# Gate and up projections of a SwiGLU by seven half-size products (Strassen's scheme) in a hybrid decoder layer

## The chip, the core and the metric

The kernel runs on one core of a Trainium2 chip. The metric is device time in microseconds of one execution; less is better. Several executions are timed, and their median counts. Beside them one execution is profiled, and all rows below are from that one. The engines are PE (TensorE), DVE (VectorE), ACT (ScalarE), POOL (GpSimd) and SP (SyncE, which here only starts transfers).

## The reference, cut to what matters

One decoder layer over 2,048 tokens of width 1,024 in float32. Two branches (a gated DeltaNet and a sliding-window attention) are merged and added to x; then comes the feed-forward part, which the change touches:

```python
x = x + merged @ w_out
h = rms_norm(x, ffn_norm)                       # (2048, 1024)
x = x + (silu(h @ w_gate) * (h @ w_up)) @ w_down  # w_gate, w_up: (1024, 2816), w_down: (2816, 1024)
```

## The kernel before

The tokens are worked off in four blocks of 512 (`TB`). Every large product keeps float32 accuracy by splitting each operand into a high part (rounded to the matmul's float32r) and the rest: a product is three matmuls, high x high, high x low, low x high (`mm3`). `weights` brings a unit of 128 x 1,024 weights in two halves of 512 columns. In block 0 it loads them raw (`wraw`), ScalarE makes the high part (L168), VectorE or GpSimd in turn the low part (L171), both into a `whl` buffer (five of them), and SP stores this pair in device memory (`wk`, L174). In blocks 1 to 3 the pair is loaded from there (L181), 512 KB for each half. L109 is the helper through which all other instructions pass.

A block runs through these stages:

- `mixer`: projections, DeltaNet and attention of the block, gates and branch outputs.
- `tok_gemm(("wo",))`: the output projection; VectorE adds it to x (eight tiles `x`).
- `norm2`: `norm_stats` scales the rows (`xn`); `norm_T` transposes them with TensorE into one bank for each 128 of the 1,024 features (k = 0 to 7), ScalarE makes the high part `h` with the gain, VectorE the low part. In blocks 0 to 2 `window_start` of the next block (the projections `skv` and `sq`, acc<-whl,h in the rows, from that block's own `hs`) is issued meanwhile.
- the feed-forward in five parts of 4, 4, 4, 4 and 6 units of 128 channels (`FSPLIT`), 22 units a block: `ffn_up` for each unit, then the down product of the part (`tok_gemm(("down", part))`, acc<-whl,a in the rows).

`ffn_up` makes gate and up of a unit with `chan_gemm`: eight steps of 128 features, three matmuls each, 512 tokens wide, into one bank; twice 24 matmuls. ScalarE takes the tanh from the bank, VectorE multiplies, ScalarE and VectorE split the result (`a`).

TensorE's order is written out by hand: `drive` issues the dense stream and puts steps of the side programs (norms, attention of the next block, DeltaNet cores) into it where an estimate says that their operands are ready; side steps have priority on the other engines. The order on these engines is fixed at build time by a scheduler that knows the buffers. Nearly all tiles of 128 x 512 (x, h, a, th and those of attention) share one pool of 63 buffers (`NU`), and there are eight accumulator banks. `hs`, the normalized input of the next block (16 buffers), stays in that pool from before the feed-forward until the next `mixer` has used it.

Of the kernel before, what the change touches and what calls it, by code (L numbers as in the profile page):

```python
# [15 lines left out]
P = 128  # L16
# [3 lines left out]
TB = 512  # L20
# [8 lines left out]
NU = 63  # L29
ND = 6  # L30
WR = 2
WB = 5
# [82 lines left out]
class Emitter:  # L115
    def __init__(self, ctx, tc, ins, out, nblocks):
# [13 lines left out]
        self.kept = {}  # L130
        self.pacc = pool("acc", 8, space=bass.MemoryType.PSUM)
# [21 lines left out]

    def weights(self, key, a):
        nc = self.raw
        n = a * 264 if key[0] == "skv" else 1024
        h = a // 2
        hl = []
        if key not in self.kept:
            src = self.w_skv[key[1]] if key[0] == "skv" else self.w_all[UNITS[key]]  # L160
            raw = self.wp.tile([P, 1056], F32, name="wraw", tag="wraw", bufs=WR)
            nc.sync.dma_start(out=raw[:, :n], in_=src)
            keep = []
            for j in range(2):
                t = self.wp.tile([P, 2, 528], F32R, name="whl", tag="whl", bufs=WB)
                r = raw[:, j * n // 2:(j + 1) * n // 2]
                hi, lo = t[:, 0, :n // 2], t[:, 1, :n // 2]
                nc.scalar.activation(hi, r, AF.Copy)  # L168
                self.nsub += 1
                eng = nc.vector if self.nsub > 6 and self.nsub % PSUB else nc.gpsimd  # L170
                eng.tensor_tensor(out=lo, in0=r, in1=hi, op=ALU.subtract)  # L171
                if self.nblocks > 1:
                    d = self.kp.tile([P, 2, n // 2], F32, name="wk", tag="wk%d_%d" % (len(self.kept), j))
                    nc.sync.dma_start(out=d, in_=t[:, :, :n // 2].bitcast(F32))  # L174
                    keep.append(d)
                hl.append([t[:, e, :n // 2].rearrange("p (a m) -> p a m", a=h) for e in range(2)])
            self.kept[key] = keep
        else:
            for j in range(2):
                t = self.wp.tile([P, 2, 528], F32R, name="whl", tag="whl", bufs=WB)  # L180
                nc.sync.dma_start(out=t[:, :, :n // 2].bitcast(F32), in_=self.kept[key][j])  # L181
                hl.append([t[:, e, :n // 2].rearrange("p (a m) -> p a m", a=h) for e in range(2)])
        return lambda k: (hl[k // h][0][:, k % h], hl[k // h][1][:, k % h])
# [914 lines left out]
```

## Time and profile before

| | |
|---|---|
| median of 3 runs | 3191.2 us (3190.91 to 3194.72) |
| the profiled execution | 3196.1 us |
| its span, first to last instruction | 3194.3 us |
| mean granted TensorE clock | 0.990 of full speed |
| data moved by transfers | 595.99 MB, 187 GB/s on average |

The span is what the trace shows; the time of the execution holds a little more around it. "Busy" is the time in which an engine has at least one instruction running, and matmuls overlap, so the distance between the starts of two matmuls is less than the duration of one. Idle time of an engine counts only where a result waits for that engine.

### The profile page before, as it was taken

How to read it: one execution, taken by the hardware profiler on the slowest of the kernel's cores; microseconds unless marked ns; L12 is line 12 of the kernel's file. 1: busy time of each engine (PE TensorE's matmuls, PEld its weight loads, DVE VectorE, ACT ScalarE, POOL GpSimd, SP SyncE). 2: the span in 40 equal slices, each digit the busy share in tenths (PEclk: the TensorE clock that was granted, in tenths of full speed). 3: DMA queues.
4: the chain of work that ended last, by engine and by line, in shares of the span. 5: the costliest groups of instructions: out<-in, count | busy, mean ns of one | idle time of the engine just before them, and what ended most of it. 6: DMA issues, size and time to landing. Idle time of an engine off the chain costs nothing. (4 is left out here: it accounts for less than half of the span.)

```text
span 3194.3 us, 39761 instructions
## 1 busy us (share of the span) xinstructions
PE 3095.3 (97%) x14854; PEld 2523.6 (79%) x14854; DVE 1403.2 (44%) x3626; ACT 837.6 (26%) x2112; POOL 415.8 (13%) x401
## 2 busy tenths in 40 slices
PE   7888989999999999999999999999999999999999
PEld 5776778778888887878887888877888888878887
DVE  5867656533336544542215565443221655422221
ACT  4454334422323322330002323232000233110000
POOL 2433211322212100010001110011000211000000
PEclk9999999999999999999999999999999999999999
DMA  6554475588874446445556445545566544645565
GB/s 240 185 178 152 154 251 209 198 284 285 283 254 145 132 142 215 153 152 191 184 192 200 131 143 179 177 154 170 190 189 205 169 131 133 198 159 193 192 189 183
DMA packets 291848, 595.99 MB, mean 187 GB/s; under 512 B 18975, under 2 KB 20168, under 8 KB 291656
## 3 DMA queue, kind: packets, MB, share of 16 engines
q1 hardware_dynamic: 277648, 569.20, 54.1%
q10 hardware_dynamic: 14008, 24.25, 2.2%
q8 instruction: 117, 1.92, 0.2%
q14 instruction: 75, 0.61, 0.1%
HBM read 459.08 MB, written 134.30 MB: 186 GB/s over the span
## 5 line engine op out<-in xcount | busy, mean ns | idle before, releaser
L109 PE MATMUL acc<-h,whl 128*128 128x512 f32 x7296 | 1760.1, 397 | 7.5 <-DVE whl L171 4.9
L109 PEld LDWEIGHTS acc<-h,whl 128*128 128x128 f32 x7296 | 1357.6, 189 | 313.9 <-DVE whl L171 5.8
L109 PE MATMUL acc<-whl,a 128*128 128x512 f32 x2112 | 493.7, 393 | 0.0
L109 PEld LDWEIGHTS acc<-whl,a 128*128 128x128 f32 x2112 | 395.5, 188 | 90.3
L109 DVE TENSOR_TENSOR x<-x,acc 128x512 f32<-128x512 f32 x192 | 131.4, 687 | 390.4 <-PE acc L109 388.6
L171 POOL TENSOR_TENSOR whl<-wraw,whl 128x512 fp32r<-128x512 f32 (+1 forms) x123 | 167.0, 1359 | 565.4 <-ACT whl L168 472.6
L168 ACT ACTIVATE whl<-wraw 128x512 fp32r<-128x512 f32 (+1 forms) x240 | 149.0, 630 | 290.3 <-PE acc L109 136.1
L109 DVE TENSOR_TENSOR th<-th,acc 128x512 f32<-128x512 f32 x88 | 60.4, 687 | 316.0 <-PE acc L109 315.8
L109 DVE SCALAR_TENSOR_TENSOR th<-th,acc 128x512 f32<-128x512 f32 x88 | 60.5, 687 | 304.9 <-ACT th L109 304.9
L109 PE MATMUL acc<-whl,mt 128*128 128x512 f32 x768 | 181.9, 398 | 8.1 <-DVE h L109 7.6
L109 ACT ACTIVATE th<-acc 128x512 f32<-128x512 f32 x88 | 52.7, 598 | 499.5 <-PE acc L109 499.3
L109 PEld LDWEIGHTS acc<-whl,mt 128*128 128x128 f32 x768 | 145.9, 191 | 43.2 <-DVE h L109 8.5
L109 DVE SCALAR_TENSOR_TENSOR cv<-xr,cst_sb,cv 128x512 f32<-128x512 f32 x144 | 134.6, 935 | 60.7 <-ACT cv L109 53.1
L109 ACT ACTIVATE a<-th 128x512 fp32r<-128x512 f32 x88 | 55.5, 631 | 346.8 <-DVE th L109 332.1
L171 DVE TENSOR_TENSOR whl<-wraw,whl 128x512 fp32r<-128x512 f32 x117 | 89.8, 768 | 121.4 <-ACT whl L168 120.9
L109 PE MATMUL acc<-whl,h 128*128 128x264 f32 (+1 forms) x768 | 139.8, 341 | 0.0
L109 PEld LDWEIGHTS acc<-whl,h 128*128 128x128 f32 x768 | 118.0, 188 | 16.7 <-issue 1.1
L109 POOL COPY ccar<-xr 128x3 f32<-128x3 f32 x48 | 9.0, 188 | 858.5 <-ACT xr L109 858.5
L109 PE MATMUL acc<-sp,whl 128*128 128x512 f32 x384 | 103.2, 409 | 0.0
L109 POOL TENSOR_TENSOR pT<-pT,cst_sb 128x512 f32<-128x512 f32 x62 | 82.7, 1362 | 137.2 <-ACT pT L109 121.1
L109 ACT ACTIVATE L<-L,ast 128x256 f32<-128x256 f32 (+1 forms) x192 | 83.4, 457 | 60.0 <-DVE ast L109 60.0
L109 PE MATMUL acc<-ydn,whl 128*128 128x512 f32 x384 | 92.6, 401 | 0.4
(183 smaller groups left out, 2817.5 us busy)
## 6 DMA issues: line engine op xcount, KB each, us to landing
whl<-wk SPq DMA_DIRECT2D x708, 512.0 KB, 3.9
wk<-whl SPq DMA_DIRECT2D x236, 512.0 KB, 3.5
wraw<-in_w_all SPq DMA_DIRECT2D x118, 512.0 KB, 5.0
x<-in_x ACTq DMA_DIRECT2D x56, 256.0 KB, 5.1
out<-x ACTq DMA_DIRECT2D x32, 256.0 KB, 3.8
whl<-wk SPq DMA_DIRECT2D x12, 528.0 KB, 5.1
wk<-whl SPq DMA_DIRECT2D x4, 528.0 KB, 2.7
x<-in_x SPq DMA_DIRECT2D x8, 256.0 KB, 6.5
```

Of the source, the lines that this page charges most:

```text
L109: r = f(*args, **kw)
L168: nc.scalar.activation(hi, r, AF.Copy)
L171: eng.tensor_tensor(out=lo, in0=r, in1=hi, op=ALU.subtract)
```

## The change

The weights of a unit are seen as four quarters: A11 and A12 are the gate's weights for features 0 to 511 and 512 to 1,023, A21 and A22 the up's. The normalized input is seen as four quarters too: B11 and B12 are features 0 to 511 for the first and the second 256 tokens, B21 and B22 features 512 to 1,023. Eight quarter products (each four steps of 128 features, 256 tokens wide) become seven, of sums:

S1 = A21 + A22, S2 = S1 - A11, S3 = A11 - A21, S4 = A12 - S2 for the weights; T1 = B12 - B11, T2 = B22 - T1, T3 = B22 - B12, T4 = B21 - T2 for the input. `ffn_up` runs them in the order S2 T2 (bank Y), A11 B11 (bank G), S1 T1 (bank Z), S3 T3 (added into Y), A12 B21 (into G), A22 T4 (into Y), S4 B22 (into Z). Between them ScalarE copies Y and G out (`c`), and VectorE and GpSimd add the pieces to gate and up.

The sums S1 to S4 are built in block 0. S1 and S2 are stored split, S3 and S4 as plain sums (256 KB); in blocks 1 to 3 S1 and S2 are loaded split, S3, S4, A11, A12 and A22 plain, and split again each time. The input sums are built in each block by `norm_S` in place of `norm_T`. All `weights` calls now load raw halves; there are five raw buffers of half a unit (before two of a whole one), six `whl` buffers and 61 buffers in the common pool. For blocks 1 to 3 `hs` is stored in device memory after `window_start` and loaded again by `refill` during the last down product of the block before.

```diff
-NU = 63
+NU = 61
 ND = 6
-WR = 2
-WB = 5
+WR = 5
+WB = 6
+KEPT_SPLIT = ("S1", "S2")
...
+    def load_raw(self, src, n=TB):
+        raw = self.wp.tile([P, 528], F32, name="wraw", tag="wraw", bufs=WR)
+        self.raw.sync.dma_start(out=raw[:, :n], in_=src)
+        return raw[:, :n]
+    def either(self):
+        self.nsub += 1
+        return self.raw.vector if self.nsub > 6 and self.nsub % PSUB else self.raw.gpsimd
+    def split_raw(self, r, n=TB):
+        t = self.wp.tile([P, 2, 528], F32R, name="whl", tag="whl", bufs=WB)
+        hi, lo = t[:, 0, :n], t[:, 1, :n]
+        self.raw.scalar.activation(hi, r, AF.Copy)
+        self.either().tensor_tensor(out=lo, in0=r, in1=hi, op=ALU.subtract)
+        return t
+    def keep(self, t, n=TB):
+        d = self.kp.tile([P, 2, n], F32, name="wk", tag="wk%d" % self.nkept)
+        self.nkept += 1
+        self.raw.sync.dma_start(out=d, in_=t[:, :, :n].bitcast(F32))
+        return d
+    def load_kept(self, d, n=TB):
+        t = self.wp.tile([P, 2, 528], F32R, name="whl", tag="whl", bufs=WB)
+        self.raw.sync.dma_start(out=t[:, :, :n].bitcast(F32), in_=d)
+        return t
...
+    def seven(self, keys):
+        quad = lambda m, h: self.w_all[UNITS[keys[m]]][:, h * TB:(h + 1) * TB]
+        own = {"A11": (0, 0), "A12": (0, 1), "A22": (1, 1)}
+        got = {}
+        first = keys not in self.kept
+        if first:
+            self.kept[keys] = {}
+        kept = self.kept[keys]
+        def sums():
+            v, gp = self.raw.vector, self.raw.gpsimd
+            for n, (m, h) in list(own.items()) + [("A21", (1, 0))]:
+                got[n] = self.load_raw(quad(m, h))
+            for n, x, y, op, eng in (("S1", "A21", "A22", ALU.add, v), ("S2", "S1", "A11", ALU.subtract, v),
+                                     ("S3", "A11", "A21", ALU.subtract, gp), ("S4", "A12", "S2", ALU.subtract, gp)):
+                got[n] = self.u([TB], name="ws")
+                eng.tensor_tensor(out=got[n], in0=got[x], in1=got[y], op=op)
+        def of(name):
+            if first:
+                if not got:
+                    sums()
+                t = self.split_raw(got[name])
+                if self.nblocks > 1 and name in KEPT_SPLIT:
+                    kept[name] = self.keep(t)
+                elif self.nblocks > 1 and name not in own:
+                    d = self.kp.tile([P, TB], F32, name="wk", tag="wk%d" % self.nkept)
+                    self.nkept += 1
+                    self.raw.sync.dma_start(out=d, in_=got[name])
+                    kept[name] = d
+            elif name in KEPT_SPLIT:
+                t = self.load_kept(kept[name])
+            else:
+                t = self.split_raw(self.load_raw(quad(*own[name]) if name in own else kept[name]))
+            return [t[:, e, :TB].rearrange("p (a m) -> p a m", a=4) for e in range(2)]
+        return of
+    def product(self, ps, w, H, operand, start=True):
+        mm = self.nc.tensor.matmul
+        for k in range(4):
+            hi, lo = H[k][operand]
+            for i, (l, r) in enumerate(((w[0], hi), (w[0], lo), (w[1], hi))):
+                mm(ps, l[:, k], r, start=start and k == 0 and i == 0, stop=k == 3 and i == 2, skip_group_check=not start)
+            yield 0
...
+    def norm_S(self, xns, gain, H):
+        nc, v, gp = self.nc, self.nc.vector, self.nc.gpsimd
+        half = (slice(0, 256), slice(256, 512))
+        for k in range(4):
+            hf = []
+            for kk in (k, k + 4):
+                ps = self.aux()
+                for t in range(NT):
+                    nc.tensor.transpose(ps[:, t * P:(t + 1) * P], xns[t][kk // 4][:, (kk % 4) * P:(kk % 4 + 1) * P], self.ident)
+                f = self.u([2, 256], name="hf")
+                nc.scalar.activation(f.rearrange("p a n -> p (a n)"), ps, AF.Copy, scale=gain[:, kk:kk + 1])
+                hf.append(f)
+                yield 0
+            (b11, b12), (b21, b22) = [(f[:, 0], f[:, 1]) for f in hf]
+            ta, tb = [self.u([2, 256], name="hs") for _ in range(2)]
+            gp.tensor_tensor(out=ta[:, 0], in0=b12, in1=b11, op=ALU.subtract)
+            gp.tensor_tensor(out=ta[:, 1], in0=b22, in1=ta[:, 0], op=ALU.subtract)
+            v.tensor_tensor(out=tb[:, 0], in0=b22, in1=b12, op=ALU.subtract)
+            v.tensor_tensor(out=tb[:, 1], in0=b21, in1=ta[:, 1], op=ALU.subtract)
+            one = self.u([2, 256], F32R, name="hb")
+            nc.scalar.activation(one[:, 0], b11, AF.Copy)
+            v.tensor_tensor(out=one[:, 1], in0=b11, in1=one[:, 0], op=ALU.subtract)
+            o = {"B11": (one[:, 0], one[:, 1])}
+            for src, names, eng in ((hf[1], ("B21", "B22"), v), (ta, ("T1", "T2"), v), (tb, ("T3", "T4"), gp)):
+                hi, lo = [self.u([2, 256], F32R, name="hb") for _ in range(2)]
+                nc.scalar.activation(hi, src, AF.Copy)
+                eng.tensor_tensor(out=lo, in0=src, in1=hi, op=ALU.subtract)
+                for i, n in enumerate(names):
+                    o[n] = (hi[:, i], lo[:, i])
+            H.append(o)
+            yield 0
...
-    def ffn_up(self, hs, f):
-        nc, v = self.nc, self.nc.vector
-        w = self.weights(("up", f, 0), 8)
-        pg = self.acc()
-        yield from self.chan_gemm(pg, w, hs)
+    def ffn_up(self, H, f):
+        nc, v, gp = self.nc, self.nc.vector, self.nc.gpsimd
+        w = self.seven((("up", f, 0), ("up", f, 1)))
+        half = (slice(0, 256), slice(256, 512))
+        bank = lambda: self.acc()[:, 0:256]
+        Y = bank()
+        yield from self.product(Y, w("S2"), H, "T2")
+        c = self.u([2, 256], name="pc")
+        nc.scalar.activation(c[:, 1], Y, AF.Copy)
+        G = bank()
+        yield from self.product(G, w("A11"), H, "B11")
+        nc.scalar.activation(c[:, 0], G, AF.Copy)
+        U = self.u([2, 256], name="pu")
+        gp.tensor_tensor(out=U[:, 0], in0=c[:, 0], in1=c[:, 1], op=ALU.add)
+        Z = bank()
+        yield from self.product(Z, w("S1"), H, "T1")
+        yield from self.product(Y, w("S3"), H, "T3", start=False)
+        v.tensor_tensor(out=U[:, 1], in0=c[:, 0], in1=Y, op=ALU.add)
         th = self.u([TB], name="th")
-        nc.scalar.activation(th, pg, AF.Tanh, scale=0.5)
-        v.scalar_tensor_tensor(out=th, in0=th, scalar=1.0, in1=pg, op0=ALU.add, op1=ALU.mult)
-        w = self.weights(("up", f, 1), 8)
-        pu = self.acc()
-        yield from self.chan_gemm(pu, w, hs)
-        v.tensor_tensor(out=th, in0=th, in1=pu, op=ALU.mult)
+        up = self.u([TB], name="up")
+        v.tensor_tensor(out=up[:, half[1]], in0=U[:, 1], in1=Z, op=ALU.add)
+        yield from self.product(G, w("A12"), H, "B21", start=False)
+        nc.scalar.activation(th[:, half[0]], G, AF.Tanh, scale=0.5)
+        v.scalar_tensor_tensor(out=th[:, half[0]], in0=th[:, half[0]], scalar=1.0, in1=G, op0=ALU.add, op1=ALU.mult)
+        yield from self.product(Y, w("A22"), H, "T4", start=False)
+        v.tensor_tensor(out=up[:, half[0]], in0=c[:, 0], in1=Y, op=ALU.add)
+        yield from self.product(Z, w("S4"), H, "B22", start=False)
+        v.tensor_tensor(out=U[:, 0], in0=U[:, 0], in1=Z, op=ALU.add)
+        nc.scalar.activation(th[:, half[1]], U[:, 0], AF.Tanh, scale=0.5)
+        v.scalar_tensor_tensor(out=th[:, half[1]], in0=th[:, half[1]], scalar=1.0, in1=U[:, 0], op0=ALU.add, op1=ALU.mult)
+        v.tensor_tensor(out=th, in0=th, in1=up, op=ALU.mult)
...
+        if b:
+            self.put = []
+            for k, h in enumerate(hs):
+                self.put.append([])
+                for e in range(2):
+                    d = self.kp.tile([P, TB], F32, name="hk", tag="hk%d_%d" % (k, e))
+                    nc = self.raw
+                    nc.scalar.dma_start(out=d, in_=h[e].bitcast(F32))
+                    self.put[-1].append(d)
+            hs.clear()
+    def refill(self, hs):
+        for d in self.put:
+            h = self.pair("h")
+            for e in range(2):
+                self.raw.scalar.dma_start(out=h[e].bitcast(F32), in_=d[e])
+            hs.append(h)
+            yield 1500
...
-        yield lambda: kv.scales
+        yield lambda: kv.scales and len(hs) == KT
...
-            yield lambda: len(h2) == KT
+            yield lambda: len(h2) == 4
...
                 last = part == len(FSPLIT) - 1
+                if last and more:
+                    h2.clear()
+                    self.spawn(self.refill(hs))
```

## Rows read from the trace of the kernel before

**Rows 1.** The page: engine, busy us, share of the span, instructions.
```profile
PE 3095.3 (97%) x14854; PEld 2523.6 (79%) x14854; DVE 1403.2 (44%) x3626; ACT 837.6 (26%) x2112; POOL 415.8 (13%) x401
```
**Rows 2.** Groups by shape, whole run: busy us, mean ns, idle before, its enders.
```profile
L109 PE MATMUL acc<-h,whl 128*128 128x512 f32 x7296 | 1760.1, 397 | 7.5 <-DVE whl L171 4.9 <-POOL whl L171 1.3 <-DVE kd L109 1.3
...
L109 PE MATMUL acc<-whl,h 128*128 128x264 f32 x384 | 47.8, 285 | 0.0
...
L109 PE MATMUL aux<-cst_sb,R 128*128 128x128 f32 x128 | 19.7, 277 | 0.0
```
**Rows 3.** Timeline of TensorE, unbroken rows of one shape: start us, us, what.
```profile
2892.80 40.44 PE L109 MATMUL acc<-h,whl 128*128 128x512 f32 x174
...
1271.78 8.45 PE L109 MATMUL acc<-whl,h 128*128 128x264 f32 x68
...
1375.99 2.22 PE L109 MATMUL aux<-kt,qT 128*128 128x256 f32 x16
...
1003.21 1.06 PE L109 MATMUL aux<-T,bl 128*128 128x128 f32 x8
```
**Rows 4.** By stretch: us, engines' busy time (instructions), granted clock, DMA share, GB/s.
```profile
528.00:587.00 59.00, 56.29 (x272) 45.48 (x271) 35.92 (x110) 30.88 (x81) 18.34 (x18) 0.97 0.61 213
...
694.00:738.00 44.00, 44.00 (x191) 35.71 (x190) 12.72 (x19) 14.04 (x24) 11.67 (x9) 1.00 0.87 297
...
1311.00:1367.00 56.00, 55.48 (x276) 44.84 (x275) 28.95 (x103) 21.83 (x64) 8.38 (x11) 1.00 0.50 160
...
1469.00:1513.00 44.00, 44.00 (x191) 35.69 (x190) 7.57 (x11) 4.29 (x7) 0.00 (x0) 1.00 0.63 196
```
**Rows 5.** Groups by shape, four units of block 3, 2890 to 2935 us.
```profile
L109 DVE TENSOR_TENSOR th<-th,acc 128x512 f32<-128x512 f32 x4 | 2.8, 688 | 16.9 <-PE acc L109 16.9
...
L109 DVE SCALAR_TENSOR_TENSOR a<-th,a 128x512 fp32r<-128x512 f32 x3 | 2.1, 692 | 2.1 <-ACT a L109 2.1
```
**Rows 6.** Groups by shape, four units of block 0, 694 to 738 us.
```profile
L171 POOL TENSOR_TENSOR whl<-wraw,whl 128x512 fp32r<-128x512 f32 x9 | 11.7, 1297 | 36.3 <-ACT whl L168 36.3
L168 ACT ACTIVATE whl<-wraw 128x512 fp32r<-128x512 f32 x17 | 10.7, 631 | 23.2 <-PE acc L109 8.4 <-issue 6.4 <-DMA wraw<-in_w_all 5.2
L171 DVE TENSOR_TENSOR whl<-wraw,whl 128x512 fp32r<-128x512 f32 x8 | 5.5, 690 | 2.9 <-ACT whl L168 2.9
```
**Rows 7.** Groups by shape, attention in block 1, 1311 to 1447 us: 256 columns from a bank.
```profile
L109 DVE CUSTOM_DVE_ANT_0 L<-aux,bias 128x256 f32<-128x256 f32 x32 | 11.6, 420 | 1.4 <-PE aux L109 1.2
```
**Rows 8.** Timeline of block 3, end of the output projection and second norm, 2800 to 2826.
```profile
2799.69 13.33 PE L109 MATMUL acc<-whl,mt 128*128 128x512 f32 x57
...
2813.06 0.69 DVE L109 TENSOR_TENSOR x<-x,acc 128x512 f32<-128x512 f32 x1 [0.70 <-PE acc L109]
...
2817.66 6.15 PE L109 MATMUL aux<-cst_sb,xn 128*128 128x128 f32 x32 [4.64 <-DVE xn L109]
...
2819.42 0.69 ACT L109 ACTIVATE h<-aux,cst_sb 128x512 fp32r<-128x512 f32 x1 [4.92 <-PE aux L109]
...
2821.98 3.04 ACT L109 ACTIVATE h<-aux,cst_sb 128x512 fp32r<-128x512 f32 x5 [0.17 <-PE aux L109]
...
2823.57 2.81 PE L109 MATMUL acc<-h,whl 128*128 128x512 f32 x11
```
**Rows 9.** Transfers in 694 to 738 and in 1469 to 1513: median us to landing last.
```profile
wraw<-in_w_all SPq DMA_DIRECT2D x8, 512.0 KB, 5.0
...
whl<-wk SPq DMA_DIRECT2D x16, 512.0 KB, 3.8
```
**Rows 10.** By stretch in block 3, columns as in rows 4.
```profile
2818.00:2820.00 2.00, 2.00 (x9) 1.52 (x9) 2.00 (x6) 0.58 (x1) 0.00 (x0) 0.50 0.03 8
...
2822.00:2824.00 2.00, 2.00 (x18) 1.96 (x17) 1.90 (x3) 2.00 (x4) 0.00 (x0) 0.97 0.00 0
```
**Rows 11.** Instructions on tile h, block 1: ns min/median/max, first and last start us.
```profile
L109 PE MATMUL acc<-h,whl x17: 387/393/404, 1311.1 to 1314.8; 128*128 128x512 f32 x17
...
L109 DVE SCALAR_TENSOR_TENSOR h<-aux,cst_sb,h x8: 741/742/745, 1288.4 to 1293.0; 128x512 fp32r<-128x512 f32 x8
```

More of the change, by code (lines that the diff above doesn't have):

```diff
@@ L130, in __init__ @@
         self.kept = {}
+        self.nkept = 0
         self.pacc = pool("acc", 8, space=bass.MemoryType.PSUM)
@@ L154, in weights @@
+    def keep(self, t, n=TB):
[7 more added lines that the diff above has]
+        return t
     def weights(self, key, a):
-        nc = self.raw
-        n = a * 264 if key[0] == "skv" else 1024
+        n = (a * 264 if key[0] == "skv" else 1024) // 2
@@ L157, in weights @@
         h = a // 2
[L158 to L171, printed above, removed]
-                if self.nblocks > 1:
[L173 to L182, printed above, removed]
@@ L183, in weights @@
-        return lambda k: (hl[k // h][0][:, k % h], hl[k // h][1][:, k % h])
+        src = self.w_skv[key[1]] if key[0] == "skv" else self.w_all[UNITS[key]]
+        hl, kept = [], []
+        for j in range(2):
+            if key in self.kept:
+                t = self.load_kept(self.kept[key][j], n)
+            else:
+                t = self.split_raw(self.load_raw(src[:, j * n:(j + 1) * n], n), n)
+                if self.nblocks > 1:
+                    kept.append(self.keep(t, n))
+            hl.append([t[:, e, :n].rearrange("p (a m) -> p a m", a=h) for e in range(2)])
@@ new lines, in weights @@
+        if kept:
+            self.kept[key] = kept
+        return lambda k: (hl[k // h][0][:, k % h], hl[k // h][1][:, k % h])
+    def seven(self, keys):
[28 more added lines that the diff above has]
+                t = self.load_kept(kept[name])
+            else:
+                t = self.split_raw(self.load_raw(quad(*own[name]) if name in own else kept[name]))
+            return [t[:, e, :TB].rearrange("p (a m) -> p a m", a=4) for e in range(2)]
+        return of
@@ L378, in norm2 @@
         yield
-        yield from self.norm_T(xns, self.g2, hs)
+        yield from self.norm_S(xns, self.g2, hs)
         yield
```

## The prediction, made before the changed kernel ran

> **What bounds the kernel now.** I read the page first: TensorE is busy for 97% of the span, VectorE for 44% [rows 1]. Busy time alone proves little, because matmuls overlap, so I went to the groups by shape. The 7,296 matmuls that multiply `whl` with `h` (4,224 of them the gate and up products) had TensorE idle for 7.5 us in front of them in all [rows 2]. The timeline gives the distance between matmul starts: 174 matmuls of 512 columns in 40.44 us; less the duration of the last one (0.39), that is 40.05 / 173 = 231.5 ns each, with no hole [rows 3]. The table by stretch shows the other engines in the same phase: in a quiet stretch of block 1, VectorE is busy 7.6 us of 44, ScalarE 4.3 and GpSimd 0; in block 0, where weights are split, 12.7, 14.0 and 11.7 [rows 4]. TensorE is the bound and it is bound by columns streamed. So a gate/up unit (one of 22 per block, 88 in all) costs 48 x 0.2315 = 11.1 us, and the 88 cost 977.9 us.
>
> **The gain.** A unit becomes seven products of 4 x 3 = 12 matmuls over 256 columns: 84 matmuls. What one costs is the main number. Four spans are at hand [rows 3]: 512 columns 231.5 ns; 264 columns (8.45 - 0.29) / 67 = 121.8 ns, with a weight load in front of each [duration in rows 2]; 256 columns (2.22 - 0.29) / 15 = 128.7 ns, in attention, where VectorE empties each bank and waits are in it; 128 columns about (1.06 - 0.28) / 7 = 111 ns, hardly less than at twice the width, so something other than columns limits there. The line through the first two has 0.442 ns a column, and 8 columns below 264 give 118.3. I take 119, nearest to the 264 row, which is the same kind of stream. After: 88 x 84 x 0.119 = 879.6 us, a gain of 98 us. Bounds: 111 ns gives 157 us, 128.7 ns gives 27 us.
> The Trainium skill (TensorE: Matmul & The Clock Gate, Part 3, "What overlaps and what doesn't") says that a weight load overlaps matmuls in flight only where it goes to another row group; here every load takes all rows, so half-size matmuls would pay each load in full. The 264-column row contradicts it: a load per matmul, and 121.8 ns. By the rule the sum is that of rival 4, by the row the one used here.
>
> **Work added on the other engines.** VectorE before, per unit: three operations of 0.69 us [rows 5] = 2.1 us, and in block 0 two of the four splits, 1.4 us [rows 6]. After: six 256-wide operations of about 0.42 [rows 7] and two 512-wide ones of 0.69: 3.9 us. Five of the seven weight operands are now split in every block, alternately by VectorE and GpSimd: 2.5 x 0.69 = 1.7 us more, 5.6 in all. In block 0 all seven are split (2.4) and two sums are built (1.4): 7.7 us. GpSimd in block 0: 3.5 splits and two sums of 1.30 [rows 6], one 256-wide add of about 0.65: 7.8 us. ScalarE in block 0: seven splits of 0.63, the tanh as two halves, two copies, one final split (0.63): 4.4 + 2.2 = 6.6. A unit lasts 84 x 0.119 = 10.0 us, so in quiet stretches every engine fits. Their work is not free where its cover is gone, in four places:
> (a) *The accumulator is read in mid-run.* Bank `Y` is read by VectorE after the fourth product, and the sixth product adds to it. Only the fifth lies between: 12 x 0.119 = 1.43 us. VectorE starts about 0.04 us after the modelled end of the last matmul (end 2799.69 + 13.33 = 2813.02, start 2813.06 [rows 8]), which lies 0.29 - 0.12 = 0.17 us after the product's last slot; its add takes 0.42. That is 0.63, leaving 0.8 us: enough for one 0.69 us operation in front, not for two. I charge 0.05 us a unit, 4 us; bounds 0 and 0.5 us a unit (44).
> (b) *Attention of the next block runs beside the first part of the feed-forward.* In block 1's stretch VectorE was busy 28.95 us of 56 [rows 4], 8.3 of them its four units. With 4 x 5.6 instead it is 43.0 of some 51.6: 83%. In block 0: 35.92 of 59, less 4 x 3.5, plus 4 x 7.7: 52.7 of 54.6, 97%. There the queue in front of (a) is long, and u-buffers (28 for the new operands, four more per unit) are as scarce as before. I charge 6 us in block 0 and 2 in blocks 1 and 2: 10; bounds 0 and 40.
> (c) *Sums of weights in block 0.* The operand `S2` of the next unit needs A21, and A21's buffer (one of five) comes free when A12 of the present unit has been split, which waits for the `whl` buffer (one of six) that is freed 1.4 us before this unit begins. From there: split 0.63 + 1.30, load 4 to 5 (512 KB took 5.0 in block 0, 3.8 later [rows 9]), S1 and S2 0.7 each, split 0.63 + 0.69 or 1.30: 8.6 to 10.3 us, of 11.4 available, queues and signals not counted. With VectorE and GpSimd about 78% busy, some waits of 0.3 us eat that. I charge 0.3 us a unit, 6 us; bounds 0 and 1.5 (33).
> (d) *The norm before the feed-forward.* It prepares 28 tiles instead of 16. ScalarE's share is five 512-wide operations per k and one half: at (3.04 - 0.69) / 4 = 0.59 us apart [rows 8], 3.25 us, for four k 13 us, against 4.7 before. In block 3 nothing covers it. There ScalarE began at 2819.42 and TensorE's first product at 2823.57 [rows 8]; the first new product needs T2 of all four k, at 2819.4 + 13 + 0.7 = 2833.1, where unhindered it would end at 2823.6 + 1.4 = 2825.0: +8 us. TensorE idles meanwhile. After the idle 4.64 us before these transposes the granted clock was 0.50, that is 1.2 GHz, and back at 2.4 GHz after 2822 [rows 8, 10]; some 5 us of work at half speed cost 2.5 us. Together 10.5; bounds 5 and 16. In blocks 0 to 2 the projections of the next block cover it: `h` was finished at 1293.0 + 0.7 and first used at 1311.1 [rows 11], 17 us of room for 8.3 more. But the 61 u-buffers do not hold everything (x1 8, xn 8, hs 16, H 28, k and v 5, four in the making: 69), so the fourth k waits until the query projection has released eight of `hs`, half way through its 96 x 0.2315 = 22 us. That still fits; 1 us each, 3; bounds 0 and 15.
>
> **Costed at nothing.** DMA: a unit of blocks 1 to 3 loads 2 x 512 + 5 x 256 KB = 2.25 MB in 10.0 us, 225 GB/s, against 2 MB in 11.1; block 0 moves 2.5 MB, 250 GB/s, and carried 297 at a share of 0.87 [rows 4]. The load of a kept operand has five products, 7.1 us, for the 3.8 of [rows 9]. If that cover went, TensorE would wait for `whl`. The 4 MB of `hs` go out during the projections and come back during the last down product (144 x 0.2315 = 33 us, so 120 GB/s, beside 12 loads of 512 KB, 190), on ScalarE's queue, where at that time nothing else is queued but the output stores, which nobody waits for. 1 us in all.
>
> **Sum.** -98 + 4 + 10 + 6 + 10.5 + 3 + 1 = -64 us. The profiled execution took 3196.1 us (span 3194.3), so 3132; the median of the runs is 4.9 us below it, so the prediction is 3127 us.
>
> **Rivals.**
> 1. *Nothing stalls.* The other engines are ordered well ahead, as in block 0 now, where VectorE's and GpSimd's splits kept TensorE idle for 4.9 + 1.3 us in all [rows 2]. For it: all averages are below 100%. Against: (a) leaves 0.8 us where before nothing on TensorE waited for an evacuation. Time: 3191 - 98 + 10 = 3103. Chance 0.17.
> 2. *The read of `Y` comes late in every unit* (the other side). VectorE is served in a fixed order; if each time two operations or one waiting split stand in front, TensorE loses about 1 us a unit. It decides from (64 + 4) / 88 = 0.77 us a unit on; at 1 us the time is 3127 - 4 + 88 = 3211, slower. For it: VectorE has eight operations a unit and 1.7 us of splits that wait for ScalarE; against: at 56% it is mostly free. Chance 0.10.
> 3. *Block 0 and the attention stretches saturate*, (b) and (c) at the upper bounds: 30 + 27 more, up to 3184; from 3150 on I count it here. Chance 0.13.
> 4. *Weight loads are not hidden at half width*, so that the change does not do what it says: 128-column step plus 256-column stream, 0.111 + 0.119 = 0.230 us, 84 x 0.230 = 19.3 us a unit, 8.2 more, 3191 + 722 = 3913. The 264-column row speaks against it. Chance 0.02. The rule of the Trainium skill named above leads here.
> My forecast, 3105 to 3150, has 0.58.
>
> **Numbers.** What measures apart from no change here is about 0.2%, 6 us. Slower: rival 2 mostly, rival 4: 0.11. Within 0.2%: the upper edge of rival 3: 0.04. Faster: the rest, 0.85. The range is 3098 (rival 1 with 118 ns and a cheaper norm) to 3186 (the edge of rival 3); it leaves out rivals 2 and 4 and a few hundredths at either end.
>
> **What the new profile must show.** 7,392 matmuls of 256 columns 119 ns apart inside a product; units of blocks 1 to 3 after attention 10.0 to 10.1 us apart; idle of TensorE in front of `acc` put down to VectorE and ScalarE, most in block 0 and the first part of blocks 1 and 2; in block 3, 10 us more between the transposes and the first product, and a second stretch at 0.50. The prediction is wrong if the 256-column step is over 125 ns, if quiet units take 10.5 us or more, or if block 0's units are no shorter than 11.1.

## The result and the profile after

The changed kernel took 3333.7 us (median of four runs, 3330.1 to 3334.5) against 3193.0 for the kernel before beside it (four runs, 3190.9 to 3195.2): ratio 1.0438, interval 1.0420 to 1.0457. It is slower by 4.4%, where 3127 us was forecast and 3186 was the upper end. The forecast failed in its sign.

The page of the changed kernel, to be held against [rows 1] (busy us, share of the span, instructions; below it the granted TensorE clock in 40 slices):

```profile
PE 3057.5 (92%) x18022; PEld 2653.0 (80%) x18022; DVE 1863.5 (56%) x4356; ACT 1164.8 (35%) x2836; POOL 892.3 (27%) x779
...
PEclk9999998878888999999999999999999999989999
```

TensorE has gone from 97% to 92%, and the slices from the seventh to the thirteenth show a lower clock. The groups by shape, and the timeline of one quiet part of four units in block 1, answer to [rows 2, 3]:

```profile
L110 PE MATMUL acc<-hb,whl 128*128 128x256 f32 x7392 | 942.8, 290 | 162.1 <-ACT whl L168 107.8 <-POOL whl L169 17.5 <-ACT pc L110 11.6
```
```profile
1635.58 39.72 PE L110 MATMUL acc<-hb,whl 128*128 128x256 f32 x336
1675.14 2.24 PE L110 MATMUL acc<-whl,a 128*128 128x512 f32 x9
```

The new matmuls run in one unbroken row, 336 in 1675.14 - 1635.58 = 39.56 us or 117.7 ns each: the scheme gives what it promises wherever TensorE isn't kept waiting. But in front of the 7,392 of them it idled for 162 us, 108 of those for a weight operand split by ScalarE, where the old products had 7.5 us in all [rows 2]. Where this happens shows when the span is cut into stages, each ending where the matmuls of the next begin (a feed-forward stage runs from the end of the output projection to the start of the next block's mixer; that of block 3 begins with its first product, so the transposes of its norm lie in the row of the mixers; the forecast is its own terms, placed by stage and rounded):

| stage | before, us | after, us | change | forecast |
|---|---|---|---|---|
| start to the end of the first output projection | 487.6 | 479.3 | -8.3 | 0 |
| feed-forward of block 0 | 439.5 | 610.2 | +170.6 | -10 |
| feed-forward of block 1 | 431.2 | 420.9 | -10.2 | -20 |
| feed-forward of block 2 | 431.2 | 426.9 | -4.4 | -20 |
| feed-forward of block 3 | 370.8 | 358.8 | -12.0 | -13 |
| the three later mixers | 1034.0 | 1032.3 | -1.7 | 0 |
| span | 3194.3 | 3328.3 | +134.0 | -64 |

Block 0 alone lost more than the whole difference. There the new operands are built from raw weights; later blocks read them back. The table by stretch (us, busy time of PE, PEld, DVE, ACT, POOL, granted clock, DMA share, GB/s) sets four units of block 0, four of block 1, and one unit of block 0 cut in four beside [rows 4]:

```profile
762.00:830.00 68.00, 47.08 (x337) 45.29 (x336) 39.05 (x54) 24.06 (x48) 36.88 (x26) 0.82 0.49 164
1635.00:1675.00 40.00, 40.00 (x339) 39.77 (x338) 21.62 (x39) 17.63 (x36) 15.65 (x13) 1.00 0.72 228
...
780.66:784.00 3.34, 3.34 (x15) 3.34 (x16) 2.21 (x2) 0.75 (x3) 3.34 (x2) 0.50 0.55 212
784.00:788.00 4.00, 4.00 (x33) 4.00 (x32) 0.00 (x0) 0.81 (x2) 2.05 (x3) 0.89 1.02 262
788.00:792.40 4.40, 4.40 (x38) 4.21 (x37) 1.69 (x4) 0.39 (x1) 1.30 (x1) 1.00 0.37 141
792.40:798.00 5.60, 0.02 (x1) 0.00 (x0) 3.52 (x6) 1.66 (x4) 0.63 (x1) 0.75 0.00 1
```

A unit of block 0 takes 17 us instead of 10, and no engine is near its limit: VectorE is busy 39 of 68 us. TensorE stands still for 5.6 us at the end of the unit, and after such a wait its matmuls begin at a granted clock of 0.50, the 1.2 GHz level, where 15 of them take 3.34 us. The timeline of that unit's end names the wait (start us, us, engine, what; in brackets the idle time before and what ended it; `ws` are the sums of weights):

```profile
780.66 11.76 PE L110 MATMUL acc<-hb,whl 128*128 128x256 f32 x82 [1.59 <-POOL whl L169]
...
782.97 2.33 SPq L158 DMA_DIRECT2D wraw<-in_w_all  x4
...
789.43 1.30 POOL L218 TENSOR_TENSOR ws<-wraw 128x512 f32<-128x512 f32 x1 [2.77 <-DMA wraw<-in_w_all]
...
792.53 0.42 DVE L110 TENSOR_TENSOR pu<-pu,acc 128x256 f32<-128x256 f32 x1 [1.07 <-PE acc L110]
...
794.61 0.63 ACT L110 ACTIVATE a<-th 128x512 fp32r<-128x512 f32 x1 [1.22 <-DVE th L110]
795.27 0.69 DVE L110 SCALAR_TENSOR_TENSOR a<-th,a 128x512 fp32r<-128x512 f32 x1 [0.69 <-ACT a L110]
795.88 0.68 DVE L218 TENSOR_TENSOR ws<-wraw 128x512 f32<-128x512 f32 x1
796.60 0.69 DVE L218 TENSOR_TENSOR ws<-ws,wraw 128x512 f32<-128x512 f32 x1
...
797.39 0.63 ACT L168 ACTIVATE whl<-ws 128x512 fp32r<-128x512 f32 x1 [2.15 <-DVE ws L218]
...
798.07 0.80 PE L110 MATMUL acc<-hb,whl 128*128 128x256 f32 x2 [5.65 <-ACT whl L168]
```

The four raw quarters of the next unit were asked for at 782.97. A21 and A11 were there at 789.43, when GpSimd built `S3` from them; A22 was asked for ahead of A21. VectorE's `S1` needs A21 and A22 and ran only at 795.88. In VectorE's order it stands behind the last operation of the present unit (`a<-th,a`, 795.27), and that hangs on the unit's last product, which ended at 792.4. So the end of one unit, two sums and a split lie in a row while TensorE has nothing to do. A part of four units has three such ends.

A second loss sits in the parts that share their time with attention. There VectorE's rows are much longer than [rows 5, 7] gave them. The groups by shape of the whole run, and a timeline in block 1:

```profile
L169 DVE TENSOR_TENSOR whl<-wraw,whl 128x512 fp32r<-128x512 f32 x271 | 232.6, 859 | 173.0 <-ACT whl L168 170.0
...
L110 DVE SCALAR_TENSOR_TENSOR th<-th,pu 128x256 f32<-128x256 f32 x88 | 57.0, 648 | 26.8 <-ACT th L110 26.8
L110 DVE TENSOR_TENSOR pu<-pc,acc 128x256 f32<-128x256 f32 x88 | 37.0, 420 | 128.8 <-PE acc L110 127.9
```
```profile
1568.82 4.43 POOL L169 TENSOR_TENSOR whl<-wraw,whl 128x512 fp32r<-128x512 f32 x3 [6.60 <-PE aux L110]
...
1569.30 1.37 DVE L169 TENSOR_TENSOR whl<-wraw,whl 128x512 fp32r<-128x512 f32 x1 [0.21 <-ACT whl L168]
...
1570.59 1.51 DVE L110 SCALAR_TENSOR_TENSOR th<-th,pu 128x256 f32<-128x256 f32 x1
...
1572.13 1.67 DVE L110 TENSOR_TENSOR th<-th,up 128x512 f32<-128x512 f32 x1
1573.72 0.68 DVE L169 TENSOR_TENSOR whl<-wraw,whl 128x512 fp32r<-128x512 f32 x1
```

While GpSimd splits (1568.82 to 1573.25), a split on VectorE takes 1.37 us, and 0.68 just after. A 256-wide product of two tiles of the on-chip buffer takes 1.51, a 512-wide one 1.67. The operation of the same width with one input in a bank of TensorE's results keeps its 420 ns on average. The Trainium skill (GPSIMD Engine Reference, "Key points") says that GpSimd shares its way into the on-chip buffer with VectorE and contends with VectorE's instructions of two such inputs. These rows agree, with 1.37, 1.51 and 1.67 us beside GpSimd.

The whole trace says the same. Of VectorE's 271 splits `whl<-wraw,whl`, the 158 during which GpSimd ran nothing took 0.69 us on average (0.675 to 0.694), and the 50 during which it ran all the time took 1.33, at worst 1.79. The experiments below give this a price.

In block 3 the norm has nothing to hide it. Stretch and timeline, beside [rows 8, 10] (`hf` are the transposed quarters, `hs` here their sums and differences, `hb` the split operands):

```profile
2961.00:2984.00 23.00, 12.35 (x44) 9.16 (x45) 18.60 (x29) 12.73 (x24) 12.52 (x12) 0.57 0.00 0
```
```profile
2961.72 8.11 PE L110 MATMUL aux<-cst_sb,xn 128*128 128x128 f32 x32 [6.02 <-DVE xn L110]
...
2976.89 1.25 ACT L110 ACTIVATE hf<-aux,cst_sb 128x512 f32<-128x512 f32 x2
...
2978.29 1.18 POOL L110 TENSOR_TENSOR hs<-hf 128x256 f32<-128x256 f32 x1
...
2979.54 0.79 POOL L110 TENSOR_TENSOR hs<-hf,hs 128x256 f32<-128x256 f32 x1
2980.36 1.15 ACT L110 ACTIVATE hb<-hs 128x512 fp32r<-128x512 f32 x2 [1.40 <-POOL hs L110]
...
2983.45 2.93 PE L110 MATMUL acc<-hb,whl 128*128 128x256 f32 x12 [1.83 <-DVE hb L110]
```

ScalarE isn't working through its five operations per k without a pause; it waits for GpSimd's two differences (1.40 us idle). The first part of block 3 takes 53.9 us, 14.3 over a quiet one, and the mean granted clock of the 23 us shown is 0.57.

### The profile page after: what moved, and what is told of

Its sections match the earlier page's. It is cut to its first block, busy times and chain, and to the rows that moved or that the text cites. A ratio compares the mean times of both kernels' runs of the same rounds, so it can differ in the third digit from the quotient of the medians.

```text
span 3328.3 us, 49444 instructions
## 1 busy us (share of the span) xinstructions
PE 3057.5 (92%) x18022; PEld 2653.0 (80%) x18022; DVE 1863.5 (56%) x4356; ACT 1164.8 (35%) x2836; POOL 892.3 (27%) x779
## 5 line engine op out<-in xcount | busy, mean ns | idle before, releaser
L110 PE MATMUL acc<-hb,whl 128*128 128x256 f32 x7392 | 942.8, 290 | 162.1 <-ACT whl L168 107.8
L110 PEld LDWEIGHTS acc<-hb,whl 128*128 128x128 f32 x7392 | 922.5, 197 | 179.4 <-ACT whl L168 112.1
L110 PE MATMUL acc<-h,whl 128*128 128x512 f32 x3072 | 772.4, 402 | 2.0 <-DVE kd L110 2.0
L110 PEld LDWEIGHTS acc<-h,whl 128*128 128x128 f32 x3072 | 567.2, 190 | 122.4 <-issue 3.2
L169 POOL TENSOR_TENSOR whl<-wraw,whl 128x512 fp32r<-128x512 f32 (+1 forms) x277 | 387.5, 1401 | 985.5 <-ACT whl L168 900.2
L168 ACT ACTIVATE whl<-wraw 128x512 fp32r<-128x512 f32 (+1 forms) x548 | 338.7, 628 | 455.1 <-PE acc L110 333.3
L169 DVE TENSOR_TENSOR whl<-wraw,whl 128x512 fp32r<-128x512 f32 x271 | 232.6, 859 | 173.0 <-ACT whl L168 170.0
L110 PEld LDWEIGHTS acc<-whl,h 128*128 128x128 f32 x768 | 120.5, 191 | 19.3 <-DMA whl<-wk 1.6
L110 POOL TENSOR_TENSOR hs<-hf 128x256 f32<-128x256 f32 x16 | 18.2, 1136 | 345.1 <-ACT hf L110 345.1
L110 DVE TENSOR_TENSOR pu<-pc,acc 128x256 f32<-128x256 f32 x88 | 37.0, 420 | 128.8 <-PE acc L110 127.9
L110 POOL TENSOR_TENSOR pT<-pT,cst_sb 128x512 f32<-128x512 f32 x62 | 85.1, 1403 | 66.9 <-ACT pT L110 65.5
L110 POOL TENSOR_TENSOR pu<-pc 128x256 f32<-128x256 f32 x88 | 76.1, 865 | 99.2 <-ACT pc L110 76.1
```

The costliest lines, as they stand in the source:

```text
L110: r = f(*args, **kw)
L168: self.raw.scalar.activation(hi, r, AF.Copy)
L169: self.either().tensor_tensor(out=lo, in0=r, in1=hi, op=ALU.subtract)
```

## The experiments

Theory A: the order of VectorE puts the sums of weights behind the end of the unit before. Rival B: the raw buffers (five) let the loads come too late. Theory C: VectorE and GpSimd slow each other.

**The sums written ahead of the end of the unit before.** Nothing is added; each unit's loads and sums are issued before the last operations of its predecessor.

```diff
...
+        of.ahead = lambda: sums() if first and not got else None
...
+        if f + 1 < NF:
+            self.pre[f + 1] = self.seven(keys(f + 1))
+            self.pre[f + 1].ahead()
         v.tensor_tensor(out=up[:, half[0]], in0=c[:, 0], in1=Y, op=ALU.add)
...
```

> The four weight sums of a unit are written ahead of the last operations of the unit before, and nothing else is changed. Theory A (place in VectorE's order: S1 and S2 stand behind the end of the previous unit, which waits for TensorE): the units of block 0 fall from 17 to 25 us to 10.5 to 12 us, TensorE's waits of 6 us a unit go, and so does most of its time at half clock; the kernel takes 3334 - 140 = about 3190 us, 3170 to 3215. Rival B (raw buffers: the loads cannot start before the splits of the present unit are done): the sums find no data at their new place, units of block 0 stay over 15 us and the kernel over 3290 us.

Measured: 3260.9 us (ratio 1.0211, 1.0195 to 1.0228). The quiet parts of block 0 went from 68.2 and 69.0 us to 47.9 and 49.4. That is A, though the time came out between the two ranges, 46 us above the one for A: the down products between the quiet parts, where the next unit's raw quarters now hold four of the five buffers, went from 22.2 to 29.5 and 28.8.

**Seven raw buffers instead of five** (room made by four in place of six small tiles).

```diff
-ND = 6
-WR = 5
+ND = 4
+WR = 7
```

> Seven raw weight buffers instead of five; the place for them is taken from the buffers of the DeltaNet part (four instead of six), which may cost some us in the stages ahead. The order of the sums stays. Theory A (order): block 0's feed-forward stays at about 560 us from its first product to its end, 3320 to 3345 us in all. Rival B (raw buffers): the loads come earlier, units of block 0 drop to 10 to 12 us, 3190 to 3230 us.

Measured: 3323.2 us, one run; the parts of block 0 stay at 68.1, 69.2 and 105.1. Rival B falls.

**All low parts on VectorE,** to take GpSimd out of the splits. VectorE gets more work by this.

```diff
-        return self.raw.vector if self.nsub > 6 and self.nsub % PSUB else self.raw.gpsimd
+        return self.raw.vector if self.nsub > 6 else self.raw.gpsimd
```

> All low parts of the weight splits are made by VectorE, none by GpSimd. Theory A adds: part of the delay in the stretches beside attention is VectorE and GpSimd slowing each other (a 256-wide add on VectorE took 1.5 us beside a GpSimd split, 0.42 alone). Then VectorE's split stays near 0.70 us instead of 0.86, the first two parts of blocks 1 and 2 gain 2 to 8 us each, block 0 loses up to 20 us or gains as much: 3300 to 3340 us. Rival (VectorE's queue length is what matters): the first two parts of blocks 1 and 2 get longer by 3 us or more each, since VectorE has 2.5 more operations a unit.

Measured: 3270.7 us (1.0246, 1.0230 to 1.0261), 63 us less than the change and better than expected. The two groups of VectorE:

```profile
L169 DVE TENSOR_TENSOR whl<-wraw,whl 128x512 fp32r<-128x512 f32 x542 | 389.2, 725 | 236.3 <-ACT whl L168 227.9
...
L110 DVE SCALAR_TENSOR_TENSOR th<-th,pu 128x256 f32<-128x256 f32 x88 | 37.0, 421 | 17.4 <-ACT th L110 17.4
```

Twice the splits on VectorE cost 389 us instead of 233, and `th<-th,pu` is back at 421 ns. Parts beside attention in blocks 1 and 2 fell from 51.3, 56.6, 53.9 and 57.7 us to 46.9, 51.2, 46.9 and 51.2. Block 0's quiet parts stay at 65.5 and 66.4: A and C are separate losses. In the profiled executions 13.5 us of what this edit gives lie ahead of the first feed-forward (479.3 to 465.8), where no new product runs.

**Only what lies around the change:** the old products and the old norm, with the new buffer counts and with `hs` stored and reloaded.

> The products, the norm and the unit's end are as before (eight steps of 512 columns), but everything around is as in the change: half-unit raw loads, five raw and six split buffers, 61 common buffers, the next block's input stored and loaded again. Theory: all that is free or better, 3180 to 3195 us (the first block's stages ahead of the feed-forward were 8 us shorter in the change). Rival: moving that input out and back costs, or the 61 buffers do: 3200 to 3230 us.

Measured: 3185.5 us (0.9976, 0.9966 to 0.9986; ten runs). The surroundings lose nothing on balance, and the first stage took 477.9 us, so what the change gained there (487.6 to 479.3) isn't owed to the seven products; the last down products of block 0 took 36.7 us instead of 33.3, the reload's first trace.

**Both repairs together:** the first edit, within a part only (so that no raw quarters wait through the down products), with the third.

```diff
...
+        if f + 1 < NF and f + 1 not in [sum(FSPLIT[:i]) for i in range(len(FSPLIT))]:
...
```

> Sums written ahead as in the first experiment, but not across the end of a part (there they held the raw buffers that the down product needed: its 22 us became 29), and all low parts on VectorE. Theory A (order) plus C (VectorE and GpSimd slow each other) say that the two gains of 73 and 63 us add: block 0's quiet units at 10.2 to 12 us, its down products back at 22 us, 3150 to 3210 us. Rival (VectorE is simply full in block 0, 3.9 + 7 x 0.69 + 1.4 = 10.1 us of a unit of 9.9): units of 13 us or more, 3215 to 3260 us.

Measured: 3176.4 us (0.9938, 0.9924 to 0.9953), faster than the kernel before by 0.6%. The two repairs together give 157 us, more than their 73 + 63: the down products between quiet parts, 29.5 and 28.8 with the first alone, are back at 22.2. The end of a unit in block 0, in VectorE's timeline:

```profile
713.69 0.42 DVE L110 TENSOR_TENSOR pu<-pc,acc 128x256 f32<-128x256 f32 x1 [2.66 <-PE acc L110]
714.15 0.42 DVE L110 TENSOR_TENSOR up<-pu,acc 128x256 f32<-128x256 f32 x1
714.49 0.68 DVE L219 TENSOR_TENSOR ws<-wraw 128x512 f32<-128x512 f32 x1
715.45 0.42 DVE L110 SCALAR_TENSOR_TENSOR th<-th,acc 128x256 f32<-128x256 f32 x1 [0.28 <-ACT th L110]
715.79 0.69 DVE L219 TENSOR_TENSOR ws<-ws,wraw 128x512 f32<-128x512 f32 x1
```
```profile
707.78:753.57 45.79, 41.60 (x338) 39.98 (x336) 38.04 (x64) 22.74 (x47) 11.67 (x10) 1.00 0.65 223
```

`S1` and `S2` (both `ws`) now run between the operations of the unit in hand, and the clock of the part is 1.00. A unit of block 0 still takes 11.4 us, with VectorE busy for 83% of it; the old products took 11.1 there, so in block 0 the scheme gains nothing even so.

**All low parts on GpSimd,** the opposite of the third (`PSUB = 1`). If C is right it must be worse than the change; if GpSimd's queue was the trouble, other rows show it.

> All low parts are made by GpSimd, the opposite of the third experiment. Theory C (the two engines slow each other): VectorE's operations with two operands in the common memory get slower still, th<-th,pu well over 0.65 us on average and th<-th,up over 0.75, the first two parts of blocks 1 and 2 stay as long or grow, 3330 to 3400 us. Rival (the length of VectorE's queue): VectorE has 1.7 us less a unit, these parts get shorter, under 3320 us.

Measured: 3410.3 us, one run, 77 us more.

```profile
L110 DVE TENSOR_TENSOR th<-th,up 128x512 f32<-128x512 f32 x88 | 106.8, 1214 | 3.0
...
L110 DVE SCALAR_TENSOR_TENSOR th<-th,pu 128x256 f32<-128x256 f32 x88 | 93.0, 1057 | 45.9 <-ACT th L110 45.9
L110 DVE TENSOR_TENSOR pu<-pc,acc 128x256 f32<-128x256 f32 x88 | 37.0, 421 | 309.2 <-PE acc L110 296.3 <-ACT whl L168 6.9 <-ACT pc L110 6.0
```

VectorE has less to do, and its operations of two on-chip tiles take 1.06 us instead of 0.42, while `pu<-pc,acc` keeps 0.42. Even the quiet parts of blocks 1 to 3 rise from 39.6 to 42.8 us. TensorE waited 46.0 us for ScalarE's copies `pc`, against 11.6 in the change: such a copy stands behind `a<-th`, which needs VectorE's slowed operations. For splits that GpSimd itself brought late it waited 27.6, against 18.1. C holds, and GpSimd's queue is a smaller part of the price.

**The norm's differences and splits on VectorE as well.** Third edit, and in the norm `gp` becomes `v` in three places.

> The third experiment, and in the second norm the two input sums and the low part that were GpSimd's go to VectorE. Theory: in block 3 the norm runs at the pace of a chain from ScalarE to GpSimd and back, 4.5 us per k, in which GpSimd's two adds take 0.8 to 0.9 us each; on VectorE the chain is 1 us or so shorter per k, block 3's first part falls from 55 to 49 to 52 us and the kernel by 3 to 7 us against the third experiment (3271). Rival (ScalarE or VectorE's own work sets the pace): the part stays at 54 us or grows.

Measured: 3268.1 us (1.0232, 1.0215 to 1.0249). The first part of block 3 fell from 55.0 to 51.4 us, as expected; the total moved by 3, inside the spread.

**Block 0 with the old products.** Block 0 uses the eight full-size products and the old norm, and builds the sums beside them for later blocks, so that nobody waits for them; low parts on VectorE.

```diff
...
-                    acts.append((yield from self.ffn_up(h2, f)))
+                    acts.append((yield from (self.ffn_up if b else self.ffn_first)(h2, f)))
...
-        yield from self.norm_S(xns, self.g2, hs)
+        yield from (self.norm_S if self.late else self.norm_T)(xns, self.g2, hs)
```

> Block 0 multiplies as before the change (eight steps of 512 columns, norm as before) and builds the four weight sums beside it, stored plain; block 1 splits S1 and S2 and stores them split; blocks 1 to 3 use seven products. All low parts on VectorE. If the loss lies in block 0's chain of sums, this removes it: block 0 costs what it did (some 267 us for its products), blocks 1 to 3 keep what the third experiment showed, 25, 25 and 13 us below the kernel before: 3120 us, 3105 to 3145. Rival (the sums hurt wherever they are built, or block 1 with seven splits a unit stalls): over 3160 us.

Measured: 3147.6 us (0.9850, 0.9835 to 0.9865), the fastest of all and 1.5% faster than the kernel before. Block 0's quiet parts are at the old 44.4. Of the 47 us gained on the kernel before, 18 lie ahead of the first feed-forward (487.6 to 469.6), where no new product runs. The kernel before with all its low parts on VectorE was not run, so what the seven products gain by themselves isn't shown.

The expectation, 3120, is missed by 28 us. Of these 12 lie in the last down products of block 0, 45.0 us instead of 33.3; 5 lie in its first part (64.2, before 59.4) and 6 in block 1, which now splits and stores `S1` and `S2` (418.4, in the third experiment 412.6):

```profile
880.83 11.71 ACTq L1066 DMA_DIRECT2D h<-hk  x16
...
892.59 2.71 ACT L168 ACTIVATE whl<-wraw 128x512 fp32r<-128x512 f32 x5 [11.14 <-DMA h<-hk]
...
893.27 7.07 PE L110 MATMUL acc<-whl,a 128*128 128x512 f32 x19 [8.43 <-ACT whl L168]
```

The 16 issues of the reload of `hs` fill ScalarE's queue for 11.7 us, and in block 0 the down weights' splits stand behind them. TensorE waits 8.4 us. Whether the queue is the cause is tried below.

**A fourth bank** for A22 x T4, so that `Y` needn't be read before it goes on; with the third edit.

```diff
-        yield from self.product(Y, w("A22"), H, "T4", start=False)
-        v.tensor_tensor(out=up[:, half[0]], in0=c[:, 0], in1=Y, op=ALU.add)
+        W = bank()
+        yield from self.product(W, w("A22"), H, "T4")
+        v.tensor_tensor(out=up[:, half[0]], in0=U[:, 1], in1=W, op=ALU.add)
```

> The third experiment (low parts on VectorE), and the product A22 T4 goes into a fourth bank and is added to what VectorE already holds, so that no product waits for VectorE's read of Y. The number of VectorE operations is the same. Theory (the read in mid-run costs in the stretches beside attention, where TensorE waited 3 to 4 us a part on VectorE's add): the first two parts of blocks 1 and 2 lose 2 to 4 us each, quiet units stay at 9.8 us; 3271 - 8 = 3263, 3255 to 3269 us. Rival (the waits come from ScalarE's copies and attention itself): no change, 3268 to 3274 us.

Measured: 3276.7 us (1.0260, 1.0243 to 1.0277), no gain on 3270.7. Attention's parts are no shorter (46.9 and 51.2 in block 1 as before the edit, 47.0 and 53.3 in block 2 where 46.9 and 51.2 stood).

**The reload issued by SyncE** instead of ScalarE (`raw.scalar` becomes `raw.sync` in `refill`), otherwise the change.

> The change with one edit: the next block's input is loaded again by transfers issued on SyncE's queue and not on ScalarE's. Theory (the 16 issues take ScalarE's queue some 12 us, and in block 0 the splits of the down weights stand behind them): the last down product of block 0 goes from 41.0 to 33 to 36 us, blocks 1 and 2, where nothing is split there, stay at 33 to 34; 3322 to 3332 us in all. Rival (the transfers compete for the memory): 41 us as before.

Measured: 3345.2 us, one run: a miss. The last down products of blocks 0, 1 and 2 took 44.4, 41.3 and 42.5 us where the change had 41.0, 33.4 and 34.2. On SyncE's queue the issues stand among the weight loads, and in block 0 the 16 of them took 12.2 us there.

**Several edits together:** old products in block 0, low parts and norm on VectorE, a fourth bank (which alone had gained nothing), and `hs` kept on chip through block 0 instead of stored and reloaded.

> Block 0 as before the change with the sums built beside it (eighth experiment), and the next block's input kept on the chip in block 0, where there is room for it; second norm on VectorE (seventh), four banks (ninth), low parts on VectorE. If the losses named are separate, they add: 3148 - 12 (the reload in block 0) - 4 (norm) - 8 (banks) = 3124 us, 3112 to 3140. Rival (they share the same waits): 3140 to 3150 us.

Measured: 3163.2 us (0.9906, 0.9891 to 0.9921), slower than with block 0 alone as before: a miss. Without the reload block 0's last down products took 34.5 us. But its first ones took 44.8 instead of 30.7, with 9.2 us of waits of TensorE in attention's steps, and the second parts of blocks 1 and 2 rose to 65.9 and 64.6, in block 1 with two waits of 4.1 and 5.0 us of TensorE for ScalarE's copy `pc`. At the first, that copy stood behind `a<-th`, which waited for VectorE's 1.48 and 1.63 us operations while GpSimd worked on attention's `pT`. Which of the added edits caused this wasn't separated.

**The reload issued by GpSimd,** with the old products in block 0 and low parts and norm on VectorE.

> The eighth experiment (block 0 as before, sums beside it, low parts on VectorE) with two edits: the next block's input is loaded again by transfers issued from GpSimd's queue, where no weight split or load stands behind them, and the second norm is on VectorE. Theory (the reload costs only through the queue that issues it): the last down product of block 0 goes from 45 to 34 to 37 us, block 3's first part from 55 to 50 to 52; 3148 - 10 - 4 = 3134 us, 3126 to 3142. Rival (the transfers themselves, or GpSimd's issuing, disturb the weight loads): 40 us or more there, 3142 to 3155 us.

Measured: 3148.2 us (0.9861, 0.9845 to 0.9878), no better than the 3147.6 of the eighth, and in the range of the rival. ScalarE is free now, yet the last down products took 46.6, 39.0 and 37.2 us, TensorE waiting for splits whose raw weights landed late. The reload costs 3 us in block 0 where all products are the old ones and 8 to 13 in the other kernels, from any of three queues, so freeing ScalarE's queue alone doesn't remove it; how much is queue and how much the transfers beside the weight loads stays open.

## Why the prediction was wrong

By stage (us, the same stages as above):

| kernel | to the first output projection | block 0 | block 1 | block 2 | block 3 |
|---|---|---|---|---|---|
| before | 487.6 | 439.5 | 431.2 | 431.2 | 370.8 |
| the change | 479.3 | 610.2 | 420.9 | 426.9 | 358.8 |
| low parts on VectorE | 465.8 | 591.1 | 412.6 | 411.9 | 357.7 |
| that and the sums ahead | 464.3 | 490.7 | 412.3 | 413.3 | 358.0 |
| old products in block 0 | 469.6 | 453.9 | 418.4 | 410.2 | 357.9 |

**The gain was right.** 88 x 84 x 0.1177 = 870.0 us instead of 879.6: 108 us, where 98 was the term. Rival 4 is dead: every one of these matmuls has its own weight load, at 117.7 ns, and the quiet units took 9.9 us where rival 4 had 19.3. The Trainium skill's rule (TensorE: Matmul & The Clock Gate, Part 3, "What overlaps and what doesn't"), by which a weight load overlaps matmuls in flight only in another row group, does not agree with this; the measurement decides.

**(c), the sums of weights in block 0, is the step that failed.** It said 8.6 to 10.3 us "of 11.4 available", charged 0.3 us a unit and bounded it by 1.5. Measured are 17.05 to 17.5 us for a unit in the quiet parts instead of 10.3: 6.7 us a unit at the least, some 148 us in 22. It followed the *data* of `S1` and `S2` (buffer, load, sum, split), found it in time, and it was: it lay ready 6.5 us before it was used. What it left out is the *place* of these sums in VectorE's order, behind the end of the unit before. That could be priced from the rows it had: after the last product come three operations of 256 columns at about 0.42, then 0.69, 0.63 and 0.69, then `S1` and `S2` at 0.69 and a split of 0.63, together 5.3 us [rows 5 to 7], where 5.65 were measured; and [rows 10] showed the clock that follows such a wait. Begun at that clock, the product run of the unit shown took 11.76 us for 82 matmuls instead of 9.65, 2.1 more. The two first edits tell it apart: placing the sums ahead gave 20 us a quiet part, more buffers nothing. Against the kernel before, the units of block 0 lost 142 us, its down products 22 and the projections in front 6. Some 8 of the 22 lie in the last one, beside the reload; what made the other 20 us wasn't separated.

**The durations of the splits were the second failure.** "Work added on the other engines" took 0.69 and 1.30 us from rows in which the two engines mostly didn't meet. The change makes them meet far more often: 37 of VectorE's splits `whl<-wraw,whl` overlapped a GpSimd instruction before, 113 after. It struck in (b): less a quiet part, and less the same difference before, the attention parts cost 12.8 us in block 1 and 16.4 in block 2 where 2 each were charged; with all low parts on VectorE, 3.6 and 3.5. With that one edit blocks 1 to 3 come to -18.6, -19.4 and -13.1, near the forecast's -20, -20 and -13. That is luck in part: the quiet units alone gave 27 us a block where the gain less (a) had 23.5, and the norm of block 3 cost more than its term.

**Terms that were mis-sized.** (d): the norm in block 3 cost 14.3 us and 2 more ahead of the first product, where 10.5 was charged and 16 was the bound; the step counted ScalarE's operations at 3.25 us per k, and the chain through GpSimd took 4.5 (2976.89 less the same row of the k before, 2972.37). With GpSimd's operations moved to VectorE 3.6 us came back. The first product didn't wait for all four k either; it began with the first and waited before each of the others. The reload, costed at 1 us because on ScalarE's queue "nothing else is queued but the output stores": in block 0 the splits are queued there, and the last down products took 41.0 us instead of 33.3. (a) stayed small: TensorE waited 9.0 us for `pu`, where 4 were charged and 44 was the bound, and a fourth bank gained nothing; so rival 2 is not what made the time longer. Rival 3 had the right places, block 0 and attention, but took its price from the bound of (c).

Of the 198 us between forecast and result, 181 lie in block 0 and 26 in blocks 1 and 2; the other stages give 9 back.

## What to carry to other kernels

When a change adds preparation for the next step, ask not only when its data is ready but behind which instruction it stands in its engine's order; if that one waits for the end of the present step, the whole chain is on the path of the bound engine. Take durations of VectorE and GpSimd from stretches where both run, and give split work to one of them where its operations read two on-chip tiles. A scheme that saves products but needs prepared weights belongs where the preparation is already done: with the low parts on VectorE, leaving the new products out of block 0 turned 2.5% slower into 1.5% faster.

## What the runs showed of the hardware that was not expected

Beside GpSimd's instructions VectorE's operations of two on-chip tiles took more than twice as long: 1.51 us instead of 0.42 for 256 columns and 1.67 instead of 0.69 for 512 in the rows shown. GpSimd slowed less: its three splits there took 4.43 us together, against 1.30 for one in [rows 6]. VectorE's operations that read a bank of results didn't slow (420 and 421 ns on average, with half or all splits on GpSimd).

Sixteen DMA issues of 256 KB in a row occupied ScalarE's queue for 11.7 us, 0.73 us each, and its compute instructions behind them waited. The same sixteen took 12.2 us on SyncE's queue.
